# MLP and FFN: up projection feature-major, down projection summed over the stage in four PSUM banks

## The chip, the cores and the metric

The kernel runs on one core of one Trainium2 chip. The metric is the device time of one execution in microseconds (us). Three timed executions of the kernel before took 1187.08, 1186.93 and 1185.76 us; their median, 1186.93 us, is the time before.

## The reference, cut to what matters

Three layers act on one sequence of 256 tokens with 1024 features. Each ends with a feed-forward stage that is added to the residual `h`. The first two are squared-ReLU MLPs of 4096 hidden features, the third is a gated FFN of 2816 hidden features:

```
def rms_norm(x, g):
    y = x * lax.rsqrt(jnp.mean(x * x, axis=-1, keepdims=True) + EPS)
    return y * g

def sq_relu_mlp(h, w_up, w_down):
    return jnp.square(jax.nn.relu(h @ w_up)) @ w_down

h = h + dsa_mixer(...)                                   # layer A
h = h + sq_relu_mlp(rms_norm(h, mlp_norm[0]), mlp_w_up[0], mlp_w_down[0])
h = h + mla_mixer(...)                                   # layer B
h = h + sq_relu_mlp(rms_norm(h, mlp_norm[1]), mlp_w_up[1], mlp_w_down[1])
x = x + merged @ w_out                                   # block 2: mLSTM and window attention
hf = rmsnorm(x, norm_ffn_g)
x = x + (jax.nn.silu(hf @ w_gate) * (hf @ w_up)) @ w_down
```

All arrays are float32.

## The kernel before, in words

The 256 tokens are two tiles `t` of 128. The residual stays in SBUF as `hres[t]` (`h_70` and `h_71` in the order of instructions), tokens on partitions. An operand of a product is kept transposed, features on partitions, as a pair of float32r parts, high and low (`xpair`, `split` at L168: ScalarE, ACT, copies the high part, VectorE, DVE, subtracts it for the low part). A weight block of 4 x 128 rows by 512 columns is one DMA of 1 MB into `raw` (three buffers), split into `whi` (ACT, L247, two halves) and `wlo` (DVE, L250, two halves); there are four buffers each of `whi` and `wlo`. A product of two such pairs is three matmuls per block of 128 rows: high by high, high by low, low by high.

`mm_tok` (L269, L270, L272) is token-major: the activations of one tile are the 128 x 128 weights of TensorE (PE), and 512 columns of `whi` or `wlo` stream past them; the output bank is 128 tokens by 512 features. `mm_feat` (L304, L305, L307) is feature-major: 128 columns of `whi` or `wlo` are the weights of the array, and 256 tokens stream; the output is 128 features by 256 tokens, two of them to a bank. Before, block 2 alone uses `mm_feat` (tiles `cv` and `qk`).

`mlp` works through eight chunks of 512 hidden features. `up` computes a chunk token-major for both tiles, takes ReLU and square on ACT (L337, L339), turns the result with four PE transposes to a bank (`transposes`, L164) and splits it into `u`. `down_proj` multiplies two chunks by `w_down`, for each output half `ci` and tile `t` in one bank `dn` (L372, L373, L375), and adds the bank to the residual (`add_res`, L312). `ffn` does the same with six chunks (the last of 256 features), two products to a chunk (gate and up) and SiLU in place of ReLU and square (L1211, L1215).

At the head of a stage `norm_x` takes the sums of squares of a tile (L174 on ACT, L176 and L155 on DVE, the power -0.5 on GpSimd, POOL, L157), multiplies the tile by the gain (`hn`, L190, or with the norm's scale too, L192) and transposes and splits it into `mx` or `fx`. With `fold=True` the scale is left out of `hn` and is applied later, as the `scale` of the ReLU or SiLU, so the transposes wait only for the residual. With `fold=False`, which block 2's mixer uses, the scale is in `hn`. `behind` queues a chunk's weight splits behind given instructions.

The program is emitted in the order of the Python code; a scheduler that simulates the engines then sets the order of each engine's instructions. Each engine executes its own queue in that order.

Of the kernel before, what the change touches and what calls it, by code (L numbers as in the profile page):

```python
# [14 lines left out]
OP = mybir.AluOpType  # L15
AX = mybir.AxisListType

P = 128
# [7 lines left out]
# Emission orders of the three mixers. An item is a piece of work (see the dictionaries `items`); *n stands for n rounds  # L26
# of the attention pipeline, ** for all that are left.
# [8 lines left out]
def constants():  # L36
    """Arrays that depend on the shapes alone: positions, masks, rope tables, bucket one-hots."""
# [52 lines left out]
def block_kernel(ctx: ExitStack, tc: tile.TileContext, a, out: bass.AP):  # L90
# [61 lines left out]
    def rsqrt_eps(ss, scale, n, eps=EPS):  # L152
        """(ss * scale + eps) ** -0.5"""
        v = sm("rv", n)
        V.tensor_scalar(v[:, :n], ss, scale, eps, op0=OP.mult, op1=OP.add)  # L155
        r = sm("rr", n)
        G.tensor_tensor(r[:, :n], v[:, :n], mhalf[:, :n], op=OP.pow)  # L157
        return r[:, :n]

    def transposes(src, n, ps=None, w=P):  # L160
        """src [128, n*w] -> PSUM [w, n*128]"""
# [17 lines left out]
    def norm_T(h, r, gain, x, t):  # L179
        """x = split transposed of h * r * gain (either may be None)"""  # L180
# [18 lines left out]
    def behind(ins):  # L199
        """what follows is queued behind ins, on their engines"""  # L200
# [5 lines left out]
    def norm_x(x, gain, fold=True):  # L206
        """x of both tiles; the instructions that weights of its products are best queued behind; what is left to scale the
        products by"""
# [10 lines left out]
    def xpair(s, kt=8):  # L219
        """an operand [features, 256 tokens] as two float32r parts, in tiles of four blocks of 128 features"""  # L220
# [9 lines left out]
    def put(x, i, t, src):  # L230
        """split src (features of tile i, 128 tokens of t) into x"""
        mark[:] = split(x[0][i][:, :, t * P:(t + 1) * P], x[1][i][:, :, t * P:(t + 1) * P], src)
# [30 lines left out]
    def mm_tok(o, x, t, parts, KT):  # L263
        """o [128 tokens, n] += x^T W, three exact partial products"""
# [17 lines left out]
    def dense_by_tile(jobs, engs=(None, None), holds=(None, None)):  # L282
        """jobs (x, KT, w, c0, n, gain, evac): all of tile 0 first, the parts of all jobs stay"""
# [14 lines left out]
    def mm_feat(o, x, parts, KT, col):  # L298
        """o [128 features, 256 tokens]"""
# [23 lines left out]

    def mlp(i):
        g = gain_row(a["mlp_norm"][i])
        x = xpair("mx")
        holds, rs = norm_x(x, g)
        us = []

        def up(cs):  # L330
            jobs = []
            for c in cs:
                u = xpair("u", 4)

                def evac(t, ps, u=u):
                    r = t2("r")
                    A.activation(r, ps, AF.Relu, scale=rs[t])  # L337
                    sq = t2("sq")
                    A.activation(sq, r, AF.Square)  # L339
                    tp = transposes(sq, 4).rearrange("p (k n) -> p k n", k=4)  # L340
                    put(u, 0, t, tp)
                jobs.append((x, 8, a["mlp_w_up"][i], c * 512, 512, None, evac))
                us.append(u)
            dense_by_tile(jobs, holds=holds[:2] if len(us) == 2 else (None, None))

        down = lambda cs, last=False: down_proj(a["mlp_w_down"][i], us, cs, last)
        up([0, 1])
        up([2])
        down([0, 1])
        up([3])  # L350
        up([4])
        down([2, 3])
        up([5])
        up([6])
        down([4, 5])
        up([7])
        down([6, 7], True)

    def down_proj(w, us, cs, by_tile):
        """residual += u W over the blocks cs of 512 features"""  # L360
        def load(ci):
            return [wparts(w, len_u(us[c]), ci * 512, 512, k0=4 * c)[0] for c in cs]

        def run(ci, pr, t):
            ps = acc("dn")
            for q, c in enumerate(cs):
                u = us[c]
                kt = len_u(u)
                _, _, (wh, wl) = pr[q]
                for k in range(kt):  # L370
                    s0 = xs(u[0], k, t)
                    PE.matmul(ps, s0, wh[:, k, :], start=(q == 0 and k == 0), stop=False)  # L372
                    PE.matmul(ps, s0, wl[:, k, :], start=False, stop=False)  # L373
                for k in range(kt):
                    PE.matmul(ps, xs(u[1], k, t), wh[:, k, :], start=False, stop=(q == len(cs) - 1 and k == kt - 1))  # L375
            add_res(t, ci, ps)
        if by_tile:
            pr = [load(ci) for ci in range(2)]
            for t in range(2):
                for ci in range(2):  # L380
                    run(ci, pr[ci], t)
        else:
            for ci in range(2):
                pr = load(ci)
                for t in range(2):
                    run(ci, pr, t)
# [4 lines left out]
    def bias_rows(coef, K, M, ohs, dst):  # L391
        """Toeplitz tables dst[h, p, s] = coef[bucket(s - p - 128), h] in DRAM"""
# [57 lines left out]
    def logits(q, k, Sk, mask=None):  # L450
        """logits [128, 2, Sk] of two heads, one bank: q holds both heads' features, k [128, 2, Sk] one head's each"""
# [6 lines left out]
    def exps(src, dst, nmx, scale, heads, l_out):  # L458
        """dst = exp(src * scale + nmx), sums to l_out; two heads"""
# [20 lines left out]
    def stages(steps, skew=(0, 1, 2)):  # L480
        """emits the stages of the steps so that a step's first stage runs ahead of the last step's later ones; one yield
        after each round"""
# [797 lines left out]
```

## Time and profile before

| | before |
|---|---|
| median of the timed executions | 1186.93 us (1185.76 to 1187.08) |
| profiled execution, span from first to last instruction | 1184.6 us |
| PE busy | 1146.9 us, 97% |
| PE weight loads (PEld) | 963.1 us, 81% |
| DVE / ACT / POOL busy | 59% / 52% / 9% |
| first MLP, first product to the next layer's transposes | 135.72 to 321.55 us |
| second MLP, the same | 441.86 to 628.31 us |
| FFN, first product to start of the last ones | 987.04 to 1177.14 us |
| DMA read and written | 194.93 MB and 6.37 MB |

The profiled execution has no time of its own on the page beside the span; the timed executions lie 1.2 to 2.5 us above it. Times in rows are us from the start of the span. A row of the timeline gives start, duration, engine, line, operation, output and inputs, shapes and how many instructions were merged (x4). Matmuls are pipelined: the duration of one is longer than the time to the start of the next, so the pace of a stream is read from the distance of starts.

### The profile page before, as it was taken

How to read it: one execution, taken by the hardware profiler on the slowest of the kernel's cores; microseconds unless marked ns; L12 is line 12 of the kernel's file. 1: busy time of each engine (PE TensorE's matmuls, PEld its weight loads, DVE VectorE, ACT ScalarE, POOL GpSimd, SP SyncE). 2: the span in 40 equal slices, each digit the busy share in tenths (PEclk: the TensorE clock that was granted, in tenths of full speed). 3: DMA queues.
4: the chain of work that ended last, by engine and by line, in shares of the span. 5: the costliest groups of instructions: out<-in, count | busy, mean ns of one | idle time of the engine just before them, and what ended most of it. 6: DMA issues, size and time to landing. Idle time of an engine off the chain costs nothing.

```text
span 1184.6 us, 15550 instructions
## 1 busy us (share of the span) xinstructions
PE 1146.9 (97%) x6004; PEld 963.1 (81%) x6004; DVE 700.7 (59%) x1216; ACT 613.1 (52%) x1072; POOL 107.9 (9%) x128
## 2 busy tenths in 40 slices
PE   7989999999988899999999999999999999999997
PEld 6747788888887788888889999889888878888886
DVE  5685555544578665545456785755474566654545
ACT  7554464453577556445446674455564435533523
POOL 1250000000039400000000000010000030000000
PEclk9979999999999899999999999999999999999999
DMA  9945455646355226465636644554554444664551
GB/s 275 301 136 102 141 179 177 199 159 199 94 146 177 89 62 206 161 219 166 200 116 201 207 162 165 176 180 139 181 174 142 163 139 160 201 225 142 178 153 61
DMA packets 110332, 197.05 MB, mean 166 GB/s; under 512 B 6580, under 2 KB 28044, under 8 KB 110260
## 3 DMA queue, kind: packets, MB, share of 16 engines
q1 hardware_dynamic: 103704, 186.90, 47.8%
q10 hardware_dynamic: 5516, 5.64, 2.0%
q0 software_dynamic: 1040, 3.54, 1.2%
q8 instruction: 47, 0.77, 0.3%
q14 instruction: 25, 0.20, 0.1%
HBM read 194.93 MB, written 6.37 MB: 170 GB/s over the span
## 4 chain that ended last, share of the span: by engine, by line
PE 87%; DVE 4%; DMA 3%; ACT 2%; issue 2%; POOL 1%; SPq 0%; ACTq 0%; POOLq 0%
PE acc L269 15%; PE acc L270 15%; PE acc L272 15%; PE dn L375 7%; PE dn L372 7%; PE dn L373 6%; PE tr L164 5%; PE po L477 3%; PE lg L453 2%; PE qk L305 2%; PE qk L304 2%; PE qk L307 2%; DMA toe_a<-vec 2%; PE cv L305 1%; PE cv L304 1%
## 5 line engine op out<-in xcount | busy, mean ns | idle before, releaser
L250 DVE TENSOR_TENSOR wlo<-raw,whi 128x1024 fp32r<-128x1024 f32 (+3 forms) x332 | 377.4, 1176 | 180.6 <-ACT whi L247 180.4
L247 ACT ACTIVATE whi<-raw 128x1024 fp32r<-128x1024 f32 (+3 forms) x340 | 324.9, 1009 | 195.1 <-PE acc L272 83.2
L157 POOL TENSOR_TENSOR rr<-rv,mhalf 128x1 f32<-128x1 f32 (+2 forms) x42 | 38.8, 924 | 820.2 <-DVE rv L155 817.7
L269 PE MATMUL acc<-whi,mxh 128*128 128x512 f32 x256 | 101.3, 397 | 0.3 <-DVE h L312 0.3
L372 PE MATMUL dn<-whi,uh 128*128 128x512 f32 x256 | 101.2, 395 | 0.0
L270 PE MATMUL acc<-wlo,mxh 128*128 128x512 f32 x256 | 100.8, 394 | 0.0
L373 PE MATMUL dn<-wlo,uh 128*128 128x512 f32 x256 | 100.8, 394 | 0.0
L269 PE MATMUL acc<-whi,cxh 128*128 128x512 f32 (+1 forms) x192 | 74.6, 389 | 0.2 <-ACT cxh L168 0.2
L272 PE MATMUL acc<-whi,mxl 128*128 128x512 f32 x256 | 72.6, 400 | 0.0
L270 PE MATMUL acc<-wlo,cxh 128*128 128x512 f32 (+1 forms) x192 | 72.4, 378 | 0.0
L269 PE MATMUL acc<-whi,fxh 128*128 128x512 f32 (+1 forms) x192 | 71.6, 379 | 0.3 <-ACT fxh L168 0.3
L270 PE MATMUL acc<-wlo,fxh 128*128 128x512 f32 (+1 forms) x192 | 71.2, 377 | 0.0
L375 PE MATMUL dn<-whi,ul 128*128 128x512 f32 x256 | 71.0, 396 | 0.0
L312 DVE TENSOR_TENSOR h<-dn,h 128x512 f32<-128x512 f32 x44 | 30.3, 689 | 52.0 <-PE dn L375 52.0
L269 PEld LDWEIGHTS acc<-whi,mxh 128*128 128x128 f32 x256 | 48.1, 188 | 11.8 <-issue 0.5
L372 PEld LDWEIGHTS dn<-whi,uh 128*128 128x128 f32 x256 | 48.1, 188 | 11.3 <-DVE h L312 0.3
L373 PEld LDWEIGHTS dn<-wlo,uh 128*128 128x128 f32 x256 | 48.1, 188 | 10.9
L270 PEld LDWEIGHTS acc<-wlo,mxh 128*128 128x128 f32 x256 | 48.1, 188 | 10.7
L375 PEld LDWEIGHTS dn<-whi,ul 128*128 128x128 f32 x256 | 47.6, 188 | 10.7
L168 DVE TENSOR_TENSOR ul<-tr,uh 128x512 fp32r<-128x512 f32 x32 | 22.0, 688 | 55.7 <-ACT uh L168 55.7
L272 PEld LDWEIGHTS acc<-whi,mxl 128*128 128x128 f32 x256 | 46.8, 188 | 9.7
L272 PE MATMUL acc<-whi,cxl 128*128 128x512 f32 (+1 forms) x192 | 50.3, 381 | 0.0
(390 smaller groups left out, 2360.0 us busy)
## 6 DMA issues: line engine op xcount, KB each, us to landing
raw<-in_w_in SPq DMA_DIRECT2D x38, 1024.0 KB
raw<-in_mlp_w_up SPq DMA_DIRECT2D x32, 1024.0 KB
raw<-in_mlp_w_down SPq DMA_DIRECT2D x32, 1024.0 KB
raw<-in_w_gate SPq DMA_DIRECT2D x10, 1024.0 KB
raw<-in_w_up SPq DMA_DIRECT2D x10, 1024.0 KB
raw<-in_w_down SPq DMA_DIRECT2D x10, 1024.0 KB
raw<-in_w_in SPq DMA_DIRECT2D x6, 688.0 KB
raw<-in_a_w_in SPq DMA_DIRECT2D x4, 1024.0 KB
```

The source lines that it names most:

```text
L157: G.tensor_tensor(r[:, :n], v[:, :n], mhalf[:, :n], op=OP.pow)
L164: PE.transpose(ps[:w, i * P:(i + 1) * P], src[:, i * w:(i + 1) * w], ident)
L247: A.activation(hi[:, c], raw[:, c], AF.Copy)
L250: (eng or V).tensor_tensor(lo[:, c], raw[:, c], hi[:, c].bitcast(F32), op=OP.subtract)
L269: PE.matmul(o, s0, wh[:, k, :], start=(g + k == 0), stop=False)
L270: PE.matmul(o, s0, wl[:, k, :], start=False, stop=False)
L272: PE.matmul(o, xs(xl, g + k, t), wh[:, k, :], start=False, stop=(g + k == KT - 1))
L304: PE.matmul(o, s0, xh[(g + k) // 4][:, (g + k) % 4, :], start=(g + k == 0), stop=False)
L305: PE.matmul(o, s0, xl[(g + k) // 4][:, (g + k) % 4, :], start=False, stop=False)
L372: PE.matmul(ps, s0, wh[:, k, :], start=(q == 0 and k == 0), stop=False)
L373: PE.matmul(ps, s0, wl[:, k, :], start=False, stop=False)
L375: PE.matmul(ps, xs(u[1], k, t), wh[:, k, :], start=False, stop=(q == len(cs) - 1 and k == kt - 1))
```

## The change

The up projection is feature-major for every chunk but the first: `up` calls `mm_feat` through `feat_bank`, two blocks of 128 features to a bank, and the bank's ReLU and square (in the FFN, SiLU and product) land with features on partitions, so that `put_feat` splits them without transposes. Chunk 0 of each stage stays token-major (`up_tok`). Since tokens are now columns, the norm's scale can't be applied to the product as a per-partition scale; `norm_x` is called with `fold=False`.

The down projection keeps one bank for each of the four pairs (`ci`, `t`) through the whole stage: three banks of the attention's pool `lg` and the one of `po`. `step(c)` adds one chunk to all four, after `up(c + 1)`; `last` adds the last two chunks and then each bank to the residual, four adds to a stage in place of 16 (MLP) and 12 (FFN). Docstrings and comments were removed, so line numbers move: `transposes` is L164 still, the new down products are L355, L356 and L358.

```
+    def feat_bank(s, x, parts, pr):
+        ps = acc(s)
+        p3 = ps.rearrange("p (e n) -> p e n", e=2)
+        for e in range(2):
+            mm_feat(p3[:, e, :], x, parts, 8, (2 * pr + e) * P)
+        return ps
+    def put_feat(u, pr, src):
+        split(u[0][0][:, 2 * pr:2 * pr + 2, :], u[1][0][:, 2 * pr:2 * pr + 2, :],
+              src.rearrange("p (k n) -> p k n", k=2))
+    def down_acc(w, us, nc_):
+        banks = {}
+        def bank(ci, t):
+            if (ci, t) not in banks:
+                banks[ci, t] = pop("dn") if (ci, t) == (1, 1) else lgp("dn")
+            return banks[ci, t]
+        def load(c, ci):
+            return wparts(w, len_u(us[c]), ci * 512, 512, k0=4 * c)[0]
+        def run(c, ci, t, part):
+            ps, u = bank(ci, t), us[c]
+            kt = len_u(u)
+            _, _, (wh, wl) = part
+            for k in range(kt):
+                s0 = xs(u[0], k, t)
+                PE.matmul(ps, s0, wh[:, k, :], start=(c == 0 and k == 0), stop=False)
+                PE.matmul(ps, s0, wl[:, k, :], start=False, stop=False)
+            for k in range(kt):
+                PE.matmul(ps, xs(u[1], k, t), wh[:, k, :], start=False, stop=(c == nc_ - 1 and k == kt - 1))
+        def step(c):
+            for ci in range(2):
+                part = load(c, ci)
+                for t in range(2):
+                    run(c, ci, t, part)
+        def last(cs):
+            parts = [[load(c, ci) for c in cs] for ci in range(2)]
+            for t in range(2):
+                for ci in range(2):
+                    for c, part in zip(cs, parts[ci]):
+                        run(c, ci, t, part)
+                    add_res(t, ci, banks[ci, t])
+        return step, last
     def mlp(i):
         g = gain_row(a["mlp_norm"][i])
         x = xpair("mx")
-        holds, rs = norm_x(x, g)
+        holds, _ = norm_x(x, g, fold=False)
         us = []
-
-        def up(cs):
-            jobs = []
-            for c in cs:
-                u = xpair("u", 4)
-
-                def evac(t, ps, u=u):
-                    r = t2("r")
-                    A.activation(r, ps, AF.Relu, scale=rs[t])
-                    sq = t2("sq")
-                    A.activation(sq, r, AF.Square)
-                    tp = transposes(sq, 4).rearrange("p (k n) -> p k n", k=4)
-                    put(u, 0, t, tp)
-                jobs.append((x, 8, a["mlp_w_up"][i], c * 512, 512, None, evac))
-                us.append(u)
-            dense_by_tile(jobs, holds=holds[:2] if len(us) == 2 else (None, None))
-
-        down = lambda cs, last=False: down_proj(a["mlp_w_down"][i], us, cs, last)
-        up([0, 1])
-        up([2])
-        down([0, 1])
-        up([3])
-        up([4])
-        down([2, 3])
-        up([5])
-        up([6])
-        down([4, 5])
-        up([7])
-        down([6, 7], True)
-
-    def down_proj(w, us, cs, by_tile):
...
+        w = a["mlp_w_up"][i]
+        def square(ps):
+            r = t2("r")
+            A.activation(r, ps, AF.Relu)
+            sq = t2("sq")
+            A.activation(sq, r, AF.Square)
+            return sq
+        def up_tok(c):
+            u = xpair("u", 4)
+            def evac(t, ps):
+                tp = transposes(square(ps), 4).rearrange("p (k n) -> p k n", k=4)
+                put(u, 0, t, tp)
+            dense_by_tile([(x, 8, w, c * 512, 512, None, evac)], holds=holds[:1])
+            us.append(u)
+        def up(c):
+            u = xpair("u", 4)
+            with behind(holds[1] if c == 1 else None):
+                parts = wparts(w, 8, c * 512, 512)
+            for pr in range(2):
+                put_feat(u, pr, square(feat_bank("up", x, parts, pr)))
+            us.append(u)
+        step, last = down_acc(a["mlp_w_down"][i], us, 8)
+        up_tok(0)
+        up(1)
+        for c in range(2, 8):
+            step(c - 2)
+            up(c)
+        last([6, 7])
...
         g = gain_row(a["norm_ffn_g_2"][0])
         x = xpair("fx")
-        holds, rs = norm_x(x, g)
+        holds, _ = norm_x(x, g, fold=False)
         us = []
+        wg, wu = a["w_gate_2"][0], a["w_up_2"][0]
+        def up_tok(c):
+            u = xpair("fu", 4)
+            sl = {}
+            def ev_gate(t, ps):
+                sl[t] = t2("silu")
+                A.activation(sl[t], ps, AF.Silu)
+            def ev_up(t, ps):
+                V.tensor_tensor(sl[t], ps, sl[t], op=OP.mult)
+                tp = transposes(sl[t], 4).rearrange("p (k n) -> p k n", k=4)
+                put(u, 0, t, tp)
+            dense_by_tile([(x, 8, wg, c * 512, 512, None, ev_gate), (x, 8, wu, c * 512, 512, None, ev_up)],
+                          holds=holds[:2])
+            us.append(u)
         def up(c):
             n = min(512, 2816 - c * 512)
-            kt = n // P
-            u = xpair("fu", kt)
-            sl = {}
-
-            def ev_gate(t, ps):
-                s_ = t2("silu")
-                A.activation(s_[:, :n], ps, AF.Silu, scale=rs[t])
-                sl[t] = s_
-
-            def ev_up(t, ps):
-                V.scalar_tensor_tensor(sl[t][:, :n], ps, rs[t], sl[t][:, :n], op0=OP.mult, op1=OP.mult)
-                tp = transposes(sl[t], kt)[:, :n].rearrange("p (k n) -> p k n", k=kt)
-                put(u, 0, t, tp)
-            dense_by_tile([(x, 8, a["w_gate_2"][0], c * 512, n, None, ev_gate),
-                           (x, 8, a["w_up_2"][0], c * 512, n, None, ev_up)],
-                          holds=holds[:2] if c == 0 else (None, None))
+            u = xpair("fu", n // P)
+            pg = wparts(wg, 8, c * 512, n)
+            pu = wparts(wu, 8, c * 512, n)
+            for pr in range(n // 256):
+                sl = t2("silu")
+                A.activation(sl, feat_bank("fg", x, pg, pr), AF.Silu)
+                ps = feat_bank("fp", x, pu, pr)
+                V.tensor_tensor(sl, ps, sl, op=OP.mult)
+                put_feat(u, pr, sl)
             us.append(u)
-        down = lambda cs, last=False: down_proj(a["w_down_2"][0], us, cs, last)
-        up(0)
+        step, last = down_acc(a["w_down_2"][0], us, 6)
+        up_tok(0)
         up(1)
-        up(2)
-        down([0, 1])
-        up(3)
-        up(4)
-        down([2, 3])
-        up(5)
-        down([4, 5], True)
+        for c in range(2, 6):
+            step(c - 2)
+            up(c)
+        last([4, 5])
```

Outside the three stages the order of instructions on PE, DVE and ACT is the same in both kernels. Three places in which it moves:

VectorE at the head of the first MLP, before; `h_71` is tile 1's residual, `hn_1225` its normed copy, `mxl` the low parts of the operand, `wlo` the splits of chunk 1:

```order
L312 TENSOR_TENSOR h_71<-acc_1128,h_71 128x512
L312 TENSOR_TENSOR h_71<-acc_1154,h_71 128x512
L168 TENSOR_TENSOR mxl_1185<-tr_1207,mxh_1183 128x4x128
L190 TENSOR_TENSOR hn_1225<-h_71,gain_1180 128x512 x2
L250 TENSOR_TENSOR wlo_1264<-raw_1262,whi_1263 128x1024 x2
L250 TENSOR_TENSOR wlo_1272<-raw_1270,whi_1271 128x1024
L176 TENSOR_TENSOR ss_1219<-ss_266_1214 128x1
```

The same place now:

```order
L312 TENSOR_TENSOR h_71<-acc_1128,h_71 128x512
L312 TENSOR_TENSOR h_71<-acc_1154,h_71 128x512
L168 TENSOR_TENSOR mxl_1185<-tr_1207,mxh_1183 128x4x128
L250 TENSOR_TENSOR wlo_1336<-raw_1334,whi_1335 128x1024 x2
L250 TENSOR_TENSOR wlo_1344<-raw_1342,whi_1343 128x1024
L176 TENSOR_TENSOR ss_1219<-ss_266_1214 128x1
L155 TENSOR_SCALAR rv_1221<-ss_1219 128x1
L250 TENSOR_TENSOR wlo_1344<-raw_1342,whi_1343 128x1024
L192 SCALAR_TENSOR_TENSOR hn_1225<-h_71,rr_1223,gain_1180 128x512 x2
```

`hn_1225` has moved behind the four halves of chunk 1's splits and behind the norm's scale `rr_1223`.

TensorE at the same place, before; `acc_1278` is chunk 0 of tile 0, `acc_1314` chunk 1 of tile 0 (operand `mxh_1182`, tile 0's part):

```order
L269 MATMUL acc_1314<-whi_1263,mxh_1182 128x512
L272 MATMUL acc_1278<-whi_1255,mxl_1185 128x512 x4
L164 MATMUL tr_1227<-ident,hn_1225 128x128 x4
L164 MATMUL tr_1235<-ident,hn_1225 128x128 x4
L270 MATMUL acc_1314<-wlo_1264,mxh_1182 128x512
L269 MATMUL acc_1314<-whi_1263,mxh_1182 128x512
L270 MATMUL acc_1314<-wlo_1264,mxh_1182 128x512
```

And now; `acc_1260` is chunk 0 of tile 0, `acc_1296` chunk 0 of tile 1, `up_1350` the first bank of chunk 1:

```order
L272 MATMUL acc_1260<-whi_1253,mxl_1185 128x512 x4
L164 MATMUL tr_1227<-ident,hn_1225 128x128 x4
L164 MATMUL tr_1235<-ident,hn_1225 128x128 x4
L269 MATMUL acc_1296<-whi_1245,mxh_1182 128x512
L270 MATMUL acc_1296<-wlo_1246,mxh_1182 128x512
L269 MATMUL acc_1296<-whi_1245,mxh_1182 128x512
L270 MATMUL acc_1296<-wlo_1246,mxh_1182 128x512
```

Behind tile 1's transposes stood products of tile 0; now the products of tile 1 stand there, which read what those transposes make.

TensorE at the head of the second MLP, before; `tr_3897` is the second half of tile 0, whose first half stands 28 rows further up, among the products of the output projection `acc_3844`:

```order
L270 MATMUL acc_3844<-wlo_3760,boh_2843 128x512
L272 MATMUL acc_3844<-whi_3759,bol_2845 128x512 x4
L164 MATMUL tr_3897<-ident,hn_3887 128x128 x4
L269 MATMUL acc_3968<-whi_3937,mxh_3872 128x512
L270 MATMUL acc_3968<-wlo_3938,mxh_3872 128x512
```

And now, with the output projection's last bank `acc_4086`:

```order
L270 MATMUL acc_4086<-wlo_4002,boh_3085 128x512
L272 MATMUL acc_4086<-whi_4001,bol_3087 128x512 x4
L164 MATMUL tr_4131<-ident,hn_4129 128x128 x4
L164 MATMUL tr_4139<-ident,hn_4129 128x128 x4
L269 MATMUL acc_4192<-whi_4177,mxh_4114 128x512
```

Both halves of tile 0 are now transposed directly ahead of the first product, which reads the first half.

## Rows read from the trace of the kernel before

**Rows 1.** The page, section 1: busy us (share of the span) and instructions of each engine
```profile
PE 1146.9 (97%) x6004; PEld 963.1 (81%) x6004; DVE 700.7 (59%) x1216; ACT 613.1 (52%) x1072; POOL 107.9 (9%) x128
```

**Rows 2.** The page, section 4: chain that ended last, shares of the span
```profile
PE 87%; DVE 4%; DMA 3%; ACT 2%; issue 2%; POOL 1%; SPq 0%; ACTq 0%; POOLq 0%
```

**Rows 3.** Windows, second MLP: length, engines' busy us (instructions), clock, DMA share, GB/s
```profile
500.00:600.00 100.00, 100.00 (x449) 81.20 (x448) 52.87 (x53) 48.96 (x60) 0.59 (x1) 1.00 0.57 186
```

**Rows 4.** The page, section 5: groups; xcount, busy us, mean ns, idle before, releaser
```profile
L269 PE MATMUL acc<-whi,mxh 128*128 128x512 f32 x256 | 101.3, 397 | 0.3 <-DVE h L312 0.3
L312 DVE TENSOR_TENSOR h<-dn,h 128x512 f32<-128x512 f32 x44 | 30.3, 689 | 52.0 <-PE dn L375 52.0
```

**Rows 5.** Timeline of PE, second MLP: start us, us, engine, line, what
```profile
473.97 0.60 PE L164 MATMUL tr<-ident,sq 128*128 128x128 f32 x4
474.32 1.17 PE L272 MATMUL acc<-whi,mxl 128*128 128x512 f32 x4
475.33 0.39 PE L269 MATMUL acc<-whi,mxh 128*128 128x512 f32 x1
...
481.36 0.40 PE L372 MATMUL dn<-whi,uh 128*128 128x512 f32 x1
...
484.15 0.39 PE L372 MATMUL dn<-whi,uh 128*128 128x512 f32 x1
```

**Rows 6.** Groups of the transposes of the hidden features, PE, by form
```profile
L164 PE MATMUL tr<-ident,sq 128*128 128x128 f32 x128 | 19.2, 272 | 0.0
...
L164 PE MATMUL tr<-ident,silu 128*128 128x128 f32 x44 | 6.7, 272 | 0.0
```

**Rows 7.** Timeline of PE, block 2's feature-major products
```profile
654.93 0.28 PE L304 MATMUL cv<-cxh,whi 128*128 128x256 f32 x1
...
656.37 0.28 PE L304 MATMUL cv<-cxh,whi 128*128 128x256 f32 x1
...
708.60 0.28 PE L304 MATMUL qk<-cxh,whi 128*128 128x256 f32 x1
...
717.12 0.28 PE L304 MATMUL qk<-cxh,whi 128*128 128x256 f32 x1
```

**Rows 8.** Timeline of PE's weight loads there
```profile
708.60 0.19 PEld L305 LDWEIGHTS qk<-cxl,whi 128*128 128x128 f32 x1
708.72 0.19 PEld L304 LDWEIGHTS qk<-cxh,whi 128*128 128x128 f32 x1
```

**Rows 9.** Timeline of PE, head of the first MLP
```profile
141.59 1.03 PE L164 MATMUL tr<-ident,hn 128*128 128x128 f32 x8
```

**Rows 10.** Timeline of ACT there
```profile
138.46 1.05 ACT L247 ACTIVATE whi<-raw 128x1024 fp32r<-128x1024 f32 x1
```

**Rows 11.** Timeline of DVE there
```profile
137.90 3.49 DVE L250 TENSOR_TENSOR wlo<-raw,whi 128x1024 fp32r<-128x1024 f32 x3
...
142.51 0.15 DVE L155 TENSOR_SCALAR rv<-ss 128x1 f32<-128x1 f32 x1
```

**Rows 12.** Timeline of PE, head of the second MLP
```profile
441.51 0.60 PE L164 MATMUL tr<-ident,hn 128*128 128x128 f32 x4
...
447.76 1.03 PE L164 MATMUL tr<-ident,hn 128*128 128x128 f32 x8
```

**Rows 13.** Timeline of ACT there
```profile
442.14 0.60 ACT L168 ACTIVATE mxh<-tr 128x512 fp32r<-128x512 f32 x1 [2.69 <-PE tr L164]
...
447.79 0.69 ACT L337 ACTIVATE r<-acc,rr 128x512 f32<-128x512 f32 x1 [0.65 <-PE acc L272]
448.40 0.60 ACT L168 ACTIVATE mxh<-tr 128x512 fp32r<-128x512 f32 x1
```

**Rows 14.** Timeline of DVE, heads of the second MLP and of the FFN
```profile
444.59 4.62 DVE L250 TENSOR_TENSOR wlo<-raw,whi 128x1024 fp32r<-128x1024 f32 x4
...
988.80 1.28 DVE L190 TENSOR_TENSOR hn<-h,gain 128x512 f32<-128x512 f32 x2
```

**Rows 15.** Timeline of PE, head of the FFN
```profile
992.99 1.04 PE L164 MATMUL tr<-ident,hn 128*128 128x128 f32 x8
```

More of the change, by code (lines that the diff above doesn't have):

```diff
@@ L346, in mlp @@
-        down = lambda cs, last=False: down_proj(a["mlp_w_down"][i], us, cs, last)
-        up([0, 1])
-        up([2])
-        down([0, 1])
-        up([3])
-        up([4])
-        down([2, 3])
-        up([5])
-        up([6])
-        down([4, 5])
-        up([7])
-        down([6, 7], True)
-    def down_proj(w, us, cs, by_tile):
[L361 to L386, printed above, removed]
```

## The prediction

> **What bounds the kernel now.** The page's first section comes first: PE is busy 97% of the span, DVE 59%, ACT 52% [rows 1]. A busy PE need not be the bound, so the chain that ended last is next: PE holds 87% of it [rows 2]. Then the stage itself: in 100 us of the second MLP PE is busy throughout at the full granted clock (1.00, the 2.4 GHz level), DVE 53, ACT 49, DMA engines 0.57 [rows 3]. The groups say the same from the other side: 256 up products had 0.3 us of idle PE ahead of them in all, while DVE stood 52.0 us idle waiting for PE before its residual adds [rows 4]. So in the three stages time is PE's issue time, and an edit is worth what it does to the distance between starts on PE. The durations don't give that: a 512-column product lasts 397 ns, but twelve of them start within 484.15 - 481.36 = 2.79 us, 232.5 ns each [rows 4, 5].
>
> **Transposes removed.** The transposes of the hidden features are 128 and 44 instructions [rows 6]: 32 sets of four in the MLPs (8 chunks, 2 tiles, 2 stages) and, in the FFN, 10 sets of four and 2 of two. Chunk 0 of each stage keeps its two sets; 28 sets go in the MLPs, 8 sets of four and the 2 of two in the FFN. A set's price is in the starts: it starts at 473.97 and the next product at 474.32, 0.35 us; the four products behind it take 475.33 - 474.32 = 1.01 us where four at pace take 0.93, so 0.08 more. That is 0.43 us a set. 36 sets of four are 15.5 us, the two halves at half price 0.4: **15.9 us removed**, all on PE, with nothing on PE to take their place [rows 5, 6].
>
> **Products in half the width.** The same columns stream, but each product of 512 becomes two of 256, each with its own weight load. Converted are 7 chunks x 48 x 2 MLPs = 672 and, in the FFN, 4 chunks x 96 = 384 (the 256-wide last chunk has 96 products of 256 in both orders): 1056 products of 512 become 2112 of 256. The trace of before has this very form in block 2: 72 starts of `qk` in 717.12 - 708.60 = 8.52 us, 118.3 ns; twelve of `cv` in 656.37 - 654.93 = 1.44 us, 120.0 ns [rows 7]. Two of them cost 236.6 against 232.5, 4.1 ns more: **4.4 us added**. The ends: nothing (exactly half of 232.5), and 240.0 - 232.5 = 7.5 ns, 7.9 us, by the `cv` row; I take the `qk` row because it is six times as long.
>
> **The unfolded norm.** Only the heads of the stages pay. Tile 0's norm is computed while the output projection still has tile 1 to do; tile 1's must be ready when chunk 0 of tile 0 ends, and before it needed neither the statistics nor to be ready so early, since products of tile 0 for a second chunk stood behind its transposes.
>
> First MLP. Chunk 0 ends and tile 1's transposes begin at 141.59 [rows 9]; two sets at 0.35 would let products go on at 142.3. But `hn` now stands on DVE behind chunk 1's splits. The third of them can't start before ACT's third copy ends, 138.46 + 1.05 = 139.51 [rows 10]; a split is 3.49 / 3 = 1.16, the two one-column operations 0.15 each, the fourth split 1.16 with POOL's power beside it: 139.51 + 1.16 + 0.30 + 1.16 = 142.1, and the first half of `hn` is there at 0.64 later, 142.8 [rows 11, 14]. From the start of a set to ACT's copy are 442.14 - 441.51 = 0.63 us, and the copy takes 0.60 [rows 12, 13]: products of tile 1 from 144.0 to 144.2 with a hop, a wait of **1.8 us**.
>
> Second MLP. Both sets of tile 0 stand directly ahead of the first product, where one was hidden earlier: the product waits for 441.51 + 0.63 + 0.60 = 442.74 instead of 442.2, 0.5 us [rows 12, 13]. Tile 1's transposes start at 447.76; behind them ACT has the ReLU of chunk 0 (to 448.48) and then the copy (to 449.00), while PE is through at 448.46: 0.6 us [rows 12, 13]. DVE's `hn` stands ahead of the 4.62 us of splits there and is not late [rows 14]. **1.1 us.**
>
> FFN. Chunk 0 has two products, so behind tile 1's transposes at 992.99 the up product of tile 0 still follows; `hn` was at 988.80 and has 4.2 us to spare [rows 14, 15]: **0**. The three heads make 2.9 us; the ends are 0 (all hidden) and 6: by the 4.62 us block of splits standing ahead of `hn` once more than I count.
>
> **Edits at nothing.** The residual adds fall by 32 of 0.69 us (24 in the MLPs, 8 in the FFN), on a DVE that was idle before them [rows 4]; ReLU and SiLU lose the scale operand; the splits of `u` read SBUF instead of PSUM; all this lies beside PE. The four persistent banks belong to the attention, which is over when a stage starts, and a step comes a full chunk (11 us of products) after the `u` it reads, so no bank or `u` is waited for. At the end of an MLP ACT has chunk 7's last ReLU behind four weight copies of 1.05, but 38 products (8.8 us) stand ahead of the first one that needs it. The weights' order changes, not their number: two blocks for each 11.2 us on PE, as before, in the same three and four buffers; the cover is DMA 0.57 and DVE 53% [rows 3]. Feature-major products need a chunk's second block after 12 products of 256 (1.4 us) instead of 12 of 512 (2.8 us); if that cover is gone, the chunks pay up to that difference, 19 chunks with 1.4 us. I take 0, because PE's idle time before chunks is 0.3 us in all [rows 4], and keep 3 us as the bad end (two chunks).
>
> **Sum.** -15.9 + 4.4 + 2.9 = -8.6 us, on a span of 1184.6. The timed executions have a median 2.3 us above that span, which the change doesn't touch: 1186.93 - 8.6 = **1178.3 us**.
>
> **Rivals.**
> *The weight loads set the pace (slower).* Twice as many loads, each 0.19 us long, are issued for the same columns. Had one to end before the next begins, 2112 products would be spaced by 190 ns, not 116: +156 us, 1330 us in all. Against it: in the trace loads start 0.12 us apart and overlap [rows 8], and the products hold 118 ns [rows 7]. For it: `qk` and `cv` are short, at other DMA load. It decides from the point where a 256-column product costs 13.0 / 2112 = 6.2 ns more than half of 232.5, 122.4 ns: there the kernel is as fast as before, and at 128 ns it takes 1199 us. The Trainium skill, "TensorE: Matmul & The Clock Gate", section "Back-to-back issue gap", says that the spacing in a stream of loads and products is set by both, about 81 ns at 128 columns and 131 ns at 512; a straight line puts 256 at 98, two of them at 1.49 of one, and by that estimate 1056 x 232.5 ns of products would grow by 121 us. This trace disagrees: 236.6 / 232.5 = 1.02.
> *Supply (no change).* The transposes were slack in which weights arrived, and PE now waits for splits or DMA instead. For it: DMA 0.57, three `raw` buffers. Against: PE hardly waits now, and 0.43 us a set is 4% of a chunk, less than the spare time of DVE and ACT [rows 3, 4]. About 1186 us.
> *The heads cost more.* A stage head stalls 2 to 3 us longer because ACT's and DVE's queues run later than in the trace of before: 1181 to 1184.
> *Transposes cost their durations.* 148 of 272 ns are 40 us [rows 6]: 1154 us. Against it are the starts [rows 5].
> *The change doesn't do what it says.* Excluded by the order of instructions: the sets of chunks 1 and up are gone, the products of 256 are there.
>
> **How the numbers follow.** No change is within 0.2%, 2.4 us, about what a measurement of this kernel can tell. My forecast, with its own range of 1174 to 1183 from the ends above (all at the good end 1171, all at the bad end 1188): 0.78. Heads so late that 1183 to 1184.5 results: 0.05; better than 1174, with the transposes' durations in it: 0.05; supply: 0.07; weight loads or another stall beyond 11 us: 0.05. Faster 0.88, same 0.07, slower 0.05.
>
> **What would show it.** After, the groups of `tr<-ident,sq` and `tr<-ident,silu` have 16 and 8 instructions. The up products start 118 to 119 ns apart (over 122: the loads pace). Each MLP lasts some 3 us less than 186 (321.55 - 135.72 before), the FFN about 2 less. PE's gap before tile 1's first product is about 1.8 us in the first MLP, 0.6 in the second, none in the FFN. Waits of PE on DVE `wlo` or on `raw` between chunks would make the prediction wrong; so would a `dn` product that waits for `uh`.

## The result, and the profile after

| | timed executions, median (range) | ratio to before, 95% interval |
|---|---|---|
| before | 1187.01 us (1185.76 to 1189.20, 4) | |
| after | 1175.84 us (1170.38 to 1177.89, 4) | 0.9898 [0.9877, 0.9919] |

The forecast was 1178.3 us, range 1174 to 1183. The profiled execution of after took 1170.38 us (span 1168.6), the fastest of its four, so the two profiles are compared stage by stage and not by their spans. The page of after, engines and chain (for [rows 1, 2]):

```profile
PE 1128.3 (97%) x6912; PEld 994.9 (85%) x6912; DVE 680.9 (58%) x1182; ACT 613.0 (52%) x1070; POOL 109.6 (9%) x128
...
PE 87%; DVE 4%; DMA 3%; ACT 2%; POOL 2%; issue 1%; SPq 0%; ACTq 0%; POOLq 0%; DVEq 0%
```

PE is 18.6 us less busy, with 908 more products and loads; part of that is clock outside the three stages, since other profiles have 1142.3 us for before and 1134.7 to 1136.1 for after. The chain is as it was. The groups of after (for [rows 4, 6]): out and in, count, busy us, mean ns, idle time before them and its releaser.

```profile
L304 PE MATMUL up<-mxh,whi 128*128 128x256 f32 x448 | 111.5, 282 | 0.0
L305 PE MATMUL up<-mxl,whi 128*128 128x256 f32 x448 | 111.2, 280 | 0.0
...
L164 PE MATMUL tr<-ident,sq 128*128 128x128 f32 x16 | 2.4, 272 | 0.0
...
L164 PE MATMUL tr<-ident,silu 128*128 128x128 f32 x8 | 1.2, 272 | 0.0
L312 DVE TENSOR_TENSOR h<-dn,h 128x512 f32<-128x512 f32 x12 | 8.3, 690 | 25.3 <-PE dn L358 25.3
```

The transposes are 16 and 8, and no up product had idle PE ahead of it. A window of the second MLP (for [rows 3]) and the pace of its up products on PE:

```profile
480.00:580.00 100.00, 100.00 (x624) 89.75 (x623) 50.47 (x47) 52.86 (x65) 0.59 (x1) 1.00 0.58 195
```
```profile
447.84 0.29 PE L304 MATMUL up<-mxh,whi 128*128 128x256 f32 x1
...
449.26 0.28 PE L304 MATMUL up<-mxh,whi 128*128 128x256 f32 x1
...
450.68 0.29 PE L304 MATMUL up<-mxh,whi 128*128 128x256 f32 x1
```

PE is busy throughout at the full clock. Twelve products start in 450.68 - 449.26 = 1.42 us, 118.3 ns each, the price that the `qk` row gave [rows 7]. By an estimate, a straight line through the figures of the Trainium skill ("TensorE: Matmul & The Clock Gate", "Back-to-back issue gap"), two of them would cost 1.49 of one of 512; here they cost 236.6 / 232.5 = 1.02.

The lengths of the stages come from starts on PE: a stage runs from its first product to the start of its last `dn` product, layer B from its first product to the second MLP's first. In us; where several profiles of one kernel differ, all are listed:

| kernel | first MLP | second MLP | FFN | layer B |
|---|---|---|---|---|
| before (2 profiles) | 185.6 | 186.2 | 190.3 | 119.0, 118.4 |
| after (4) | 184.2, 184.1, 185.3, 184.1 | 182.0 | 187.4 | 116.0, 116.9, 116.9, 117.0 |
| unfold | 186.4 | 186.2 | 190.3 | 118.3 |
| halves | 187.7 | 186.3 | 193.2 | 116.9 |
| tok_acc | 189.7 | 186.6 | 190.3 | 119.1 |
| feat_pair | 185.4 | 182.8 | 188.1 | 116.9 |
| dummy_tr | 190.3 | 188.1 | 187.4 | 117.2 |
| hold2 (3) | 181.8 | 182.0 | 187.4 | 119.5, 119.6, 119.4 |

In the first pair of profiles the three stages are 1.42, 4.25 and 2.90 us shorter, 8.6 in all. The mean of all timed executions fell from 1185.94 (80) to 1175.45 us (23), by 10.5 with a standard error of 0.6.

### The profile page after: what moved, and what is told of

Same layout as the page of the kernel before. It is cut to its first block, busy times and chain, and to the rows that moved or that the text cites. A ratio compares the mean times of both kernels' runs of the same rounds, so it can differ in the third digit from the quotient of the medians.

```text
span 1168.6 us, 17282 instructions
## 1 busy us (share of the span) xinstructions
PE 1128.3 (97%) x6912; PEld 994.9 (85%) x6912; DVE 680.9 (58%) x1182; ACT 613.0 (52%) x1070; POOL 109.6 (9%) x128
## 4 chain that ended last, share of the span: by engine, by line
PE 87%; DVE 4%; DMA 3%; ACT 2%; POOL 2%; issue 1%; SPq 0%; ACTq 0%; POOLq 0%; DVEq 0%
PE acc L269 8%; PE acc L270 8%; PE acc L272 8%; PE dn L356 7%; PE dn L355 7%; PE dn L358 7%; PE up L304 5%; PE up L307 5%; PE up L305 5%; PE tr L164 3%; PE po L503 3%; PE lg L479 2%; PE qk L305 2%; PE qk L304 2%; PE qk L307 2%; DMA toe_a<-vec 2%
## 5 line engine op out<-in xcount | busy, mean ns | idle before, releaser
L304 PE MATMUL up<-mxh,whi 128*128 128x256 f32 x448 | 111.5, 282 | 0.0
L305 PE MATMUL up<-mxl,whi 128*128 128x256 f32 x448 | 111.2, 280 | 0.0
L356 PE MATMUL dn<-wlo,uh 128*128 128x512 f32 x256 | 100.6, 394 | 0.0
L355 PE MATMUL dn<-whi,uh 128*128 128x512 f32 x256 | 100.2, 393 | 0.0
L304 PEld LDWEIGHTS up<-mxh,whi 128*128 128x128 f32 x448 | 84.3, 188 | 0.7
L305 PEld LDWEIGHTS up<-mxl,whi 128*128 128x128 f32 x448 | 84.3, 188 | 0.7
L307 PE MATMUL up<-mxh,wlo 128*128 128x256 f32 x448 | 71.2, 281 | 0.0
L358 PE MATMUL dn<-whi,ul 128*128 128x512 f32 x256 | 69.6, 394 | 0.0
L307 PEld LDWEIGHTS up<-mxh,wlo 128*128 128x128 f32 x448 | 60.6, 188 | 0.0
L358 PEld LDWEIGHTS dn<-whi,ul 128*128 128x128 f32 x256 | 48.1, 188 | 11.2
L355 PEld LDWEIGHTS dn<-whi,uh 128*128 128x128 f32 x256 | 48.1, 188 | 10.6
L356 PEld LDWEIGHTS dn<-wlo,uh 128*128 128x128 f32 x256 | 48.1, 188 | 10.6
L168 DVE TENSOR_TENSOR ul<-sq,uh 128x512 fp32r<-128x512 f32 x28 | 19.4, 692 | 51.2 <-ACT uh L168 50.8
L304 PE MATMUL qk<-cxh,whi 128*128 128x256 f32 x192 | 49.1, 287 | 0.0
L305 PE MATMUL qk<-cxl,whi 128*128 128x256 f32 x192 | 48.3, 282 | 0.0
L487 ACT ACTIVATE lg<-lg,nx 128x128 f32<-128x128 f32 (+1 forms) x80 | 35.5, 446 | 17.3 <-DVE nx L547 16.7
```

Of the source, the lines that this page charges most:

```text
L304: PE.matmul(o, s0, xh[(g + k) // 4][:, (g + k) % 4, :], start=(g + k == 0), stop=False)
L305: PE.matmul(o, s0, xl[(g + k) // 4][:, (g + k) % 4, :], start=False, stop=False)
L307: PE.matmul(o, wl[:, k, col:col + P], xh[(g + k) // 4][:, (g + k) % 4, :], start=False, stop=(g + k == KT - 1))
L355: PE.matmul(ps, s0, wh[:, k, :], start=(c == 0 and k == 0), stop=False)
```

## The experiments

The ratios are to before.

**Both kernels again.** No edit: how far do the stages repeat, and what varies?

> The kernel before, unchanged, against itself. Between the two traces the three stages account for 8.3 us; the other 7.7 us of the spans' difference lie in layers A and B, whose instructions the change leaves in order. Theory (the granted clock of layers A and B differs from execution to execution whatever the kernel): ratio 1.000 within 0.004, some executions with a mean granted clock of 0.99 or more, and those 4 to 8 us shorter than those at 0.987. Rival (the change itself moves the clock there): every execution near 0.987 and within 2 us of 1187.

> The changed kernel, unchanged, again. Theory of clock by chance: ratio about 0.993 where the clocks of both are alike, executions between 1170 and 1179 us by their granted clock, and in the profile the stages as long as in the first one (first MLP 184.2, second 182.0, FFN 187.4 us, each within 0.3) while layers A and B differ by some us. Rival: layers A and B repeat their short times (mlp head at 131.6 us).

Measured: before 0.9995 [0.9981, 1.0010], after 0.9919 [0.9904, 0.9933]; two later repeats of after 0.9917 [0.9887, 0.9947] and 0.9921 [0.9893, 0.9949]. The stages repeat to 0.1 us, with one exception in the first MLP (the last section). What varies is layers A and B, whose instructions are the same in both kernels: of the repeat of before, the three executions with a mean granted clock of 0.993 took 1181.1 to 1182.8 us and the eight at 0.987 took 1186.3 to 1188.9. So the clock varies without the change, as the theory said.

**dummy_tr: put the transposes back.** After, with four transposes that nothing reads for each feature-major bank of the MLPs, 14 sets to an MLP:

```
-                put_feat(u, pr, square(feat_bank("up", x, parts, pr)))
+                sq = square(feat_bank("up", x, parts, pr))
+                transposes(sq, 4)
+                put_feat(u, pr, sq)
```

> The changed kernel with four transposes of every square of the MLPs' feature-major banks put back, into a bank that nothing reads: 28 sets, the number that the change took out of the MLPs. Theory (a set costs 0.43 us of TensorE's issue time): each MLP 6.0 us longer, 12.0 us in all, ratio to the changed kernel 1.010. Rival (the transposes ran in slack): under 4 us.

Measured: 1188.0 us, 1.0014 [1.0001, 1.0028], 12.2 us above the 1175.84 of after; the MLPs are 6.11 and 6.12 us longer than after's, 0.437 us a set. A set on PE in this kernel:

```profile
460.79 0.60 PE L164 MATMUL tr<-ident,sq 128*128 128x128 f32 x4
461.14 0.37 PE L305 MATMUL up<-mxl,whi 128*128 128x256 f32 x1
461.35 0.64 PE L307 MATMUL up<-mxh,wlo 128*128 128x256 f32 x4
```

The set takes 0.35 us of starts, and the product behind it 461.35 - 461.14 = 0.21 in place of 0.118. The 0.43 of the forecast holds; the durations (4 x 272 ns) are no price.

**halves: the price of half the width alone.** Before, with every token-major up product of the three stages done as two of 256 columns, so 1248 products of 512 become 2496 (cut):

```
-                mm_tok(ps[:, :n], x, t, pr, KT)
+                for a0 in range(0, n, 256 if halves else n):
+                    a1 = min(n, a0 + (256 if halves else n))
+                    half = [(g, kk, (wh[:, :, a0:a1], wl[:, :, a0:a1])) for g, kk, (wh, wl) in pr]
+                    mm_tok(ps[:, a0:a1], x, t, half, KT)
```

> The kernel before, with each token-major up product of 512 columns (1536 to 2112 weight loads more for the same columns: all up chunks of 512) done as two of 256, first half of the bank first, then the other. 768 products of each MLP pair (768) and 480 of the FFN become 2496. Theory (a half costs 118.3 ns by the feature-major products of before): 1248 x 4.1 ns = 5.1 us longer, ratio 1.004. Rival (weight loads set the pace): above 122 ns each, over 14 us longer, ratio 1.012 or more.

Measured: 1190.91 us, 1.0044 [1.0026, 1.0062]; the stages 2.08, 0.09 and 2.91 longer, 5.1 us, as 1248 times 4.1 ns gives. The sum agrees and the shares don't (1.6, 1.6 and 2.0 were expected): the halves start 118.5, 116.8 and 119.6 ns apart in the three stages, in the mean over all that don't follow a transpose. Why the second MLP's are the closest stays open. The loads don't set the pace.

**unfold: the norm's scale in `hn` alone.** Before, with the scale moved (the MLPs' part; the FFN likewise):

```
-        holds, rs = norm_x(x, g)
+        holds, _ = norm_x(x, g, fold=False)
...
-                    A.activation(r, ps, AF.Relu, scale=rs[t])
+                    A.activation(r, ps, AF.Relu)
```

> The kernel before with the norm's scale put into the normed tile in all three stages, nothing else: two token-major chunks still stand at each head. Theory (tile 0's 11 us of products cover the statistics): the heads cost 0 to 0.6 us each, stages as before within 0.6 us, ratio 1.000 within 0.002. Rival (the unfolded norm itself costs about 1 us a head, with any cover): 2 to 4 us longer.

Measured: 1187.73 us, 1.0015 [1.0003, 1.0026]; the first MLP 0.8 longer, the others as before. DVE runs the splits of chunk 1 ahead of `hn` here as in after, but PE has a second chunk of tile 0 to do meanwhile. So the late norm costs little as long as two chunks of tile 0 stand in front of tile 1; the wait of after needs the one chunk ahead together with the unfolded norm and, as hold2 shows, the splits in front of `hn`.

**feat_pair and tok_acc: the two halves of the change apart.** feat_pair has the feature-major up projection with the down projection of before (pairs of chunks, 44 residual adds). tok_acc has the persistent banks and the unfolded norm with all chunks token-major. Both edits are to after, both are cut to the MLPs' part, and feat_pair comes first:

```
-        step, last = down_acc(a["mlp_w_down"][i], us, 8)
+        w_d = a["mlp_w_down"][i]
...
+        up(2)
+        down_proj(w_d, us, [0, 1], False)
...
```
```
-        up(1)
+        up_tok(1)
...
-            up(c)
+            up_tok(c)
...
```

> The feature-major up projection alone: the down projection as before, two chunks at a time, in the pool of two banks that the up products use as well, with 16 and 12 residual adds. Theory (the gain is the up projection's): stages as in the changed kernel within 1 us each, ratio to before as the changed kernel's within 0.002. Rival (banks shared by up and down stall the products, as the adds and the squares must free them): 3 us or more longer than the changed kernel.

> The down projection's persistent banks and the unfolded norm alone: all chunks stay token-major with their transposes, one chunk at a time. Theory (only transposes and width move TensorE's time): as before, apart from the heads: 2 to 4 us longer than before, ratio 1.002 to 1.004. Rival (the persistent banks give something, by fewer residual adds or a freer order): shorter than before by 2 us or more.

Measured: feat_pair 1176.89 us, 0.9915 [0.9891, 0.9940]; tok_acc 1191.20 us, 1.0033 [1.0015, 1.0051]. The gain is the up projection's. The banks add something on top of it only: with pairs the second MLP and the FFN are 0.8 and 0.7 us longer than after, and in each of them one `dn` product waits for a residual add to free its bank (feat_pair, PE):

```profile
610.43 0.23 PE L939 MATMUL cwT<-ident,cw 80*128 80x80 f32 x1
610.91 0.50 PE L433 MATMUL dn<-whi,uh 128*128 128x512 f32 x1 [0.25 <-DVE h L312]
...
1160.23 0.50 PE L433 MATMUL dn<-whi,fuh 128*128 128x512 f32 x1 [0.32 <-DVE h L312]
```

By the starts that is some 0.45 us each; the rest of the 0.8 and 0.7 is not located. Behind the second MLP, 0.23 us of after's gain is lost again, since its block 2 starts that much later behind the last product. tok_acc's first MLP pays 4.1 us, read in the last section.

**hold2: the splits of chunk 1 behind tile 1's norm.** After, with one index changed:

```
-            with behind(holds[1] if c == 1 else None):
+            with behind(holds[2] if c == 1 else None):
```

> The changed kernel with chunk 1's weight splits of each MLP queued behind tile 1's operand instead of tile 0's. Theory (in the first MLP TensorE's wait of 2.4 us ahead of tile 1's transposes is made by the splits that stand ahead of the normed tile on VectorE): that wait falls below 0.5 us, the first MLP is 1.5 to 2.4 us shorter (about 182 us), the second within 0.5, ratio to the changed kernel 0.998. Rival (the chain of statistics alone is too long): more than 1.5 us of the wait stays.

Measured: 1175.97 us, 0.9912 [0.9893, 0.9931]. The first MLP is 2.3 us shorter than after's. The head in after, PE, DVE, POOL:

```profile
136.30 1.09 PE L272 MATMUL acc<-whi,mxl 128*128 128x512 f32 x4
139.62 1.29 PE L164 MATMUL tr<-ident,hn 128*128 128x128 f32 x8 [2.23 <-DVE hn L192]
140.94 0.50 PE L269 MATMUL acc<-whi,mxh 128*128 128x512 f32 x1
```
```profile
132.98 3.73 DVE L250 TENSOR_TENSOR wlo<-raw,whi 128x1024 fp32r<-128x1024 f32 x3 [0.26 <-ACT whi L247]
136.63 0.15 DVE L176 TENSOR_TENSOR ss<-ss 128x1 f32<-128x1 f32 x1
136.81 0.15 DVE L155 TENSOR_SCALAR rv<-ss 128x1 f32<-128x1 f32 x1
137.04 1.23 DVE L250 TENSOR_TENSOR wlo<-raw,whi 128x1024 fp32r<-128x1024 f32 x1
138.73 1.41 DVE L192 SCALAR_TENSOR_TENSOR hn<-h,rr,gain 128x512 f32<-128x512 f32 x2 [0.46 <-POOL rr L157]
```
```profile
137.05 1.64 POOL L157 TENSOR_TENSOR rr<-rv,mhalf 128x1 f32<-128x1 f32 x1 [24.47 <-DVE rv L155]
```

The same places in hold2, PE, DVE, POOL:

```profile
139.52 1.04 PE L164 MATMUL tr<-ident,hn 128*128 128x128 f32 x8
140.86 0.50 PE L269 MATMUL acc<-whi,mxh 128*128 128x512 f32 x1 [0.30 <-ACT mxh L168]
```
```profile
136.49 1.42 DVE L192 SCALAR_TENSOR_TENSOR hn<-h,rr,gain 128x512 f32<-128x512 f32 x2 [0.67 <-POOL rr L157]
```
```profile
135.90 0.56 POOL L157 TENSOR_TENSOR rr<-rv,mhalf 128x1 f32<-128x1 f32 x1 [21.03 <-DVE rv L155]
```

In after PE has nothing from 136.30 + 4 x 0.2325 = 137.23 to 139.62, and the first product of tile 1 comes at 140.94. Eight transposes in a row took 142.38 - 141.59 = 0.79 us in before, where nothing had to be waited for behind them ([rows 9] and the product that followed):

```profile
142.38 0.48 PE L270 MATMUL acc<-wlo,mxh 128*128 128x512 f32 x1
```

Beyond these 0.79, after has 140.94 - 137.23 - 0.79 = 2.9 us of waiting and hold2 140.86 - 139.52 - 0.79 = 0.55. So the stage is 2.3 us shorter, and yet the whole time is after's: layer B is 2.7 to 3.6 us longer than in the two profiles of after by then, in instructions that are the same. Two more runs of each were made to see whether that is chance:

> hold2 once more: the splits of chunk 1 stand behind the third hold, so that tile 1's normed copy comes first. Outside layers A and B it took 969.8 us against 972.0. Theory (clock by chance): median span 1172 to 1173, 0.9980 to 0.9983 of the changed kernel. Rival (the order of the splits shifts the clock in A and B): 1174 to 1175, no difference to the changed kernel; A and B together then lie near 204 in this profile and 202 in the changed kernel's.

> The changed kernel once more, beside hold2, to see whether the 2.4 us that hold2 takes out of the first MLP are in the whole time. What lies outside layers A and B (three stages, block 2) is the same in every execution of this kernel, 972.0 us in both profiles so far; layers A and B together took 196.7 and 203.2 us at granted clocks that differ. Theory: the clock in A and B is drawn by execution and knows nothing of the code, so over many executions A and B average alike in both kernels: median span 1174 to 1175.5, about 2.2 above hold2's. Rival: the changed kernel's A and B run at a better clock than hold2's by 1.5 us or more (202.7 against 204.4 so far in the medians of 10 and 6 executions), and the two whole times stay within 0.7 us.

Measured: hold2 1172.80 us, 0.9901 [0.9874, 0.9929], and 1174.99, 0.9916 [0.9889, 0.9943]. Over all executions hold2's mean is 1174.25 us (18), after's 1175.45 (23): 1.2 less with a standard error of 0.8, which excludes neither the 2.2 of the theory nor the rival's nothing. The profiles say more: layer B took 119.4 to 119.6 in all three of hold2 and 116.0 to 117.0 in all four of after. So in these profiles the time of layer B goes with the kernel, against the theory that chance alone sets it; whether it does in the executions without a profile is not shown. Layer B in before, after and the second run of hold2, from 40 to 60 and from 60 to 90 us behind its first product; the third number from the end is the granted clock:

```profile
362.83:382.83 20.00, 17.77 (x102) 15.37 (x101) 18.15 (x43) 16.77 (x42) 18.02 (x25) 0.91 0.48 156
382.83:412.83 30.00, 25.16 (x148) 22.41 (x147) 19.25 (x42) 15.08 (x40) 16.20 (x20) 0.89 0.27 88
```
```profile
357.29:377.29 20.00, 16.96 (x104) 14.79 (x103) 18.65 (x43) 16.62 (x42) 18.93 (x26) 1.00 0.46 154
377.29:407.29 30.00, 26.18 (x173) 23.50 (x171) 20.53 (x48) 16.03 (x44) 15.43 (x19) 0.94 0.27 88
```
```profile
357.01:377.01 20.00, 17.74 (x102) 15.45 (x101) 18.15 (x43) 16.74 (x42) 18.36 (x25) 0.91 0.45 155
377.01:407.01 30.00, 26.10 (x147) 23.63 (x146) 18.97 (x42) 15.07 (x40) 15.89 (x20) 0.83 0.26 88
```

Before and hold2 lose the clock to the 1.2 GHz level for part of the first stretch, after doesn't. The first stretch is at 1.00 in all seven profiles in which layer B took 116.0 to 117.2 us (after, feat_pair, halves, dummy_tr), and at 0.91 in all seven in which it took 118.3 to 119.6 (before, unfold, tok_acc, hold2). The start of layer B doesn't decide it (317.0 in this run of hold2, 317.3 in after). What does stays open.

## Why the prediction was right, and where it was off

**The mechanism and the sum.** PE's issue time was the bound, and the stages lost 8.6 us against a forecast of 8.6. The sign of some 3 us less for each MLP came as 1.4 and 4.25. The two large terms were priced right: a set of transposes 0.437 us for 0.43 (dummy_tr), a product of half the width 118.3 ns (pace of after; 5.1 us for 1248 in halves). All the rivals but the late heads are out: no wait on `wlo` or `raw` between chunks, none of a `dn` product for `uh`, no pace set by loads, no price by durations.

**The heads, the term that was mis-sized.** The forecast gave the first MLP a wait of 1.8 us, counted from 142.3; counted from 142.38, where products went on in before, it is 1.7. Measured are 2.9. Of the 1.2 between them, 0.46 is the idle time of DVE ahead of `hn`, which waited for POOL's power: the forecast let the fourth split run "with POOL's power beside it", but the power took 1.64 us there, against 0.56 in hold2. Another 0.4 is the third split, which ended 0.5 us ahead of PE (136.71 against 137.23) where the forecast had 0.9 (140.67 against 141.59); 0.25 the way from the start of `hn` to the transposes, 0.89 for 0.64; 0.1 the statistics and the fourth split. hold2, which only moves the splits, takes out 2.4 of the 2.9.

The second MLP was right. Its two waits, after, PE:

```profile
431.97 1.04 PE L164 MATMUL tr<-ident,hn 128*128 128x128 f32 x8
433.26 0.50 PE L269 MATMUL acc<-whi,mxh 128*128 128x512 f32 x1 [0.25 <-ACT mxh L168]
...
438.97 1.04 PE L164 MATMUL tr<-ident,hn 128*128 128x128 f32 x8
440.30 0.50 PE L269 MATMUL acc<-whi,mxh 128*128 128x512 f32 x1 [0.30 <-ACT mxh L168]
```

Beyond the 0.79 of eight transposes they are 0.50 and 0.54 us (forecast 0.5 and 0.6); the first falls ahead of the stage as it is cut here. The FFN pays nothing at its head, as forecast.

**Why the sum still came out: luck.** Without the heads the terms give each MLP 14 x 0.43 - 336 x 4.1 ns = 4.6 us and the FFN 2.3. Measured, with the waits of tile 1 put back: 1.42 + 2.9 = 4.3, 4.25 + 0.54 = 4.8, and 2.90. The differences (-0.3, 0.2 and 0.6) and the 0.5 of the second MLP's first wait, which falls into layer B, make up for the 1.1 by which the first head exceeds its 1.8: the sum is right to 0.1 us by offsetting misses.

Most of the first and the third difference is the price of the width. The forecast took one price, 232.5 ns, from `dn` products, for every product of 512 columns. The mean distance of starts of up products that don't follow a transpose is 231.6, 233.0 and 233.2 ns in the three stages of before; of the products of 256 in after it is 118.5, 118.6 and 118.2. So two halves cost 5.4, 4.2 and 3.2 ns more than one whole, 1.8, 1.4 and 1.2 us in place of 1.4, 1.4 and 1.6. The FFN's last chunk, 256 wide in both kernels, went from 119.2 to 118.2 ns a product (0.1 us), the `dn` products became 0.2 to 0.5 ns closer (about 0.1 us a stage), and a set of transposes was worth 0.437 and not 0.43 (0.1 us an MLP). Why these paces differ by stage is not shown.

**The rest, 1.9 us.** The time fell by 10.5 in the mean, the stages by 8.6. Layer B is 2.0 us shorter in the mean of its profiles (118.7 against 116.7), though it now carries a wait of 0.50; that is the clock in a stage whose instructions didn't change, and the forecast had no term for it. But layer A, up to the first product of the first MLP, is 1.4 us longer in the same profiles (135.6 against 134.2), and it ranges from 131.6 to 137.4 in the four of after alone. So that layer B makes up the 1.9, and with it most of the 2.5 us by which the time lies below 1178.3, is plausible and not shown.

## What to carry to other kernels

Price an edit on a saturated engine by the distance of starts, the instruction behind it included, and take the price from the same form elsewhere in the trace: both held here to 0.01 us and 1 ns in the changed kernel. When an edit lets an operand be needed one chunk earlier, follow its whole chain through every engine, and put bulk work that shares an engine with it behind it; one index gave back 2.3 us of the first MLP, though the whole time doesn't show it clear of the clock. Compare stages rather than spans, and read the granted clock of the stages that were not touched before crediting or blaming the edit for them.

## What the runs showed of the hardware

**POOL waits for DVE's splits.** The one-column power took 1.64 or 1.65 us in the first MLP's head of each profile in which a DVE split of 1.23 us started with it (all of after, unfold, tok_acc, feat_pair, dummy_tr), and 0.56 in before, halves and hold2, where none ran; in after it ended 138.69 - 138.27 = 0.42 us behind the split. The Trainium skill, "SBUF — State Buffer", section "SBUF: two separate sides", says that a VectorE operation with two SBUF inputs and a GpSimd operation that reads SBUF shut each other out for a whole instruction. The rows agree.

**A wait of 2.3 us can cost the clock as well.** In seven profiles (all of after, feat_pair, tok_acc, dummy_tr) PE stands idle for 2.3 to 2.4 us ahead of tile 1's transposes. In three of them (the third of after, feat_pair, tok_acc) the clock fell to the 1.2 GHz level when PE went on. Ten us at this place, in after and in the third profile of after; the granted clock is again the third number from the end:

```profile
136.60:141.60 5.00, 2.71 (x15) 1.73 (x14) 3.66 (x8) 2.83 (x5) 1.64 (x1) 1.00 0.94 321
141.60:146.60 5.00, 5.00 (x26) 4.19 (x25) 2.27 (x4) 2.60 (x3) 0.00 (x0) 1.00 0.25 96
```
```profile
141.08:146.08 5.00, 2.84 (x13) 2.16 (x12) 3.23 (x7) 2.28 (x5) 1.65 (x1) 0.80 0.93 333
146.08:151.08 5.00, 5.00 (x22) 4.16 (x22) 1.75 (x3) 1.97 (x3) 0.00 (x0) 0.86 0.21 82
```

The transposes and the next product in the latter last 1.90 and 0.79 us, against 1.29 and 0.50 above:

```profile
144.04 1.90 PE L164 MATMUL tr<-ident,hn 128*128 128x128 f32 x8 [2.16 <-DVE hn L192]
145.78 0.79 PE L269 MATMUL acc<-whi,mxh 128*128 128x512 f32 x1
```

That first MLP took 185.3 us in place of 184.1 to 184.2, so the drop cost 1.1 to 1.2 us. It accounts for feat_pair's 185.4, and for tok_acc's 4.1 us over before as about 2.9 of wait and 1.2 of clock. None of hold2's three profiles shows it. Why the other four keep the clock stays open.
